# One pass of all 512 tokens up to the gates, in place of a pass of 128 tokens and a pass of 384

## The chip, the cores and the metric

One NeuronCore of one Trainium2 chip runs the whole layer. The metric is the device time of one execution in microseconds (us); of several runs the median counts.

## The reference

One layer of a streaming encoder, 512 tokens, model width 2048, all in float32:

```
h      = rms_norm(x)
proj   = h @ w_in                    # conv value, conv gate, q, k, v, gate_conv, gate_attn
conv   = silu(layer_norm(depthwise31(value * sigmoid(gate)))) @ w_conv_out
attn   = band_attention(rms(q), rms(k), v, rel_bias) @ w_attn_o
x      = x + (sigmoid(gate_conv) * conv + sigmoid(gate_attn) * attn) @ w_out
h2     = rms_norm(x)
idx, g = top 16 of 128 x 128 product keys, 8 heads, of h2 @ w_query
x      = x + sum_k g_k * gelu(h2 . expert_u[idx_k]) * expert_v[idx_k]
```

The convolution is causal over 31 taps, and the attention looks back 8 chunks of 64 tokens, so later tokens need values of earlier ones.

## The kernel before

The weights are streamed as some 640 pieces (**subs**) of 512 rows by 512 columns (1 MB) or 384 columns (0.75 MB, q, k and v of one head). `Net.run` goes through them in one order: for sub i it issues the load of a later sub on SP (tile `raw`), splits sub i+1 into a rounded high part `whi` (ACT, L121) and the rest `wlo` (DVE, L122), and issues the matmuls of sub i (`mm_sub`, L156): weight high by activation high, high by low, and low by high, 48 matmuls for one 1 MB sub where the tokens are the moving columns (`add_fm`), 12 where 128 tokens stand still and the weight's 512 columns move (`add_tm`). Behind each sub it pops background work from a queue with a budget: convolution taps, top-k, routing (`run_bg`), and **gather steps** from a second queue `gq` at a rate per sub (`grate`). A gather step fetches 128 rows of 8 KB of `expert_u` or `expert_v` with an indirect DMA on POOL (L1295) and then multiplies or accumulates them on DVE (L1322, L1330). There are 384 of them: 256 for the first 128 tokens, 128 for the last 64. The 320 tokens between go another way: all of `expert_u` and `expert_v` is streamed as weights (`ut`, `vt`).

The stages in program order:

- A, 128 tokens, 192 subs: convolution input (up to L428), q, k and v with plain float32 matmuls on weights that aren't split (`native`, L342), gates, then conv_out, attn_o, w_out and the query projection (L561 to L641). Its weight loads use five buffers, two of them in the pool `wpx` (L104), and run up to five subs ahead (L135).
- B, the other 384 tokens, 192 subs: b (convolution input), c (q, k, v and the attention, 16 heads), d (gates), e (conv_out), f (attn_o), g (w_out), i (query). The convolution's last 30 inputs and the keys and values of A come back through `cy_d` and `kv_d`. From here on three raw buffers are used. The top-k and routing of the first 128 tokens run in the background of b and c, and their gathers follow.
- k: `expert_u` by 320 tokens, 128 subs, with the routing of those tokens beside it (`place`, L1252, and `g_d`).
- m: `expert_v` by 320 tokens, 128 subs, with two 640 KB loads (`gt`, `gel`) for each four subs; then `finish_x` (L1344 on).

What `gq` still holds behind the last sub is run there, before `finish_x`:

```python
    N.run()
    while N.gq:
        N.gq.popleft()()
    finish_x()
```

Of the kernel before, what the change touches and what calls it, by code (L numbers as in the profile page):

```python
# [11 lines left out]
F32 = mybir.dt.float32  # L12
# [11 lines left out]
P = 128  # L24
# [19 lines left out]
UPB = 7  # L44
BUD_B = 4.4
BUD_C = 3.2
# [3 lines left out]
G_B, G_C, G_D, G_E, G_I, G_K, G_M = 0.4, 0.5, 1.1, 1.6, 0.6, 1.05, 1.15  # L50
URATE = 1.15
BUD_A, BUD_N = 0.5, 2.3
# [8 lines left out]
class Net:  # L61
    def __init__(self, nc, tc, A):
        self.nc, self.tc, self.A = nc, tc, A
        self.bg, self.late = deque(), deque()
        self.gq = deque()
        self.uq = deque()
        self.gacc, self.grate, self.credit, self.uacc = 0.0, G_B, 0.0, 0.0
        self.subs = []
# [22 lines left out]
    def add(self, src, ncol, mm, pre=None, post=None, budget=8.0, native=False):  # L91
        self.subs.append((src, ncol, mm, pre, post, budget, native))

    def run(self):
# [7 lines left out]
        def load(i):  # L102
            src, ncol = self.subs[i][:2]
            pool, bufs = (self.wpx, 2) if i < self.na and i % 5 > 2 else (self.wp, 3)  # L104
            raw = pool.tile([P, 4, ncol], F32, tag="raw", name="raw", bufs=bufs)
            for a, b in pieces(i):
                if i == 0:
                    self.beside(a)
                nc.sync.dma_start(raw[:, a:b, :], src[:, a:b, :])
            raws[i] = raw  # L110

        def split(i):
            raw = raws.pop(i)
            ncol = self.subs[i][1]
            if self.subs[i][6]:
                splits[i] = (raw, None)
                return
# [10 lines left out]
        for i in range(n):  # L128
            src, ncol, mm, pre, post, budget, native = self.subs[i]
# [57 lines left out]
def build(nc, tc, A):  # L187
# [4 lines left out]
    gp = es.enter_context(tc.tile_pool(name="gp", bufs=1))  # L192
    actp = []
# [4 lines left out]
    def act_tile(name):  # L198
        return actp[-1].tile([P, 4, T], F32R, tag="act", name=name, bufs=8)
# [23 lines left out]
    cy_d = drp.tile([P, 16, PAD], F32, name="cy_d")  # L223
    kv_d = [drp.tile([P, 4, 4, TA], F32, name=f"kvd{g}") for g in range(4)]
# [33 lines left out]
    def resplit(src4, goff, kg, rinv, new, name, n=T):  # L258
# [30 lines left out]
    io128f = gp.tile([P, 4, W], F32, tag="gat", name="io128f", bufs=3)[:, 0, :P]  # L289
# [17 lines left out]
    def blocks(t):
        return t.rearrange("p a (b c) -> p (a b) c", b=4)

    def wtmp(name):  # L310
        return pa.tile([P, W], F32, tag="wt", name=name, bufs=2)

    def small(n):
        return lambda name: pa.tile([P, n], F32, tag=f"{name}{n}", name=name, bufs=2 if n < TA else 1)

    nop = lambda: None

    def quad(c):
        return slice(4 * c, 4 * c + 4)

    def turned(src, then):

        def go():
            bank = psx.tile([P, 4, P], F32, tag="aux", name="tq", bufs=3)
            for k in range(4):
                nc.tensor.transpose(bank[:, k, :], src[:, k * P:k * P + P], ident)
            then(bank)
        pend.extend((nop, go))

    def add_tm(src, act, evac, nchunk, ncol=W, pre=None, budget=BUD_A, native=False, post=None):  # L330

        st = {}
        for c in range(nchunk):
            for kg in range(KG):
                def mm(hi, lo, c=c, kg=kg):
                    if kg == 0:
                        st[c] = psa.tile([P, W], F32, tag="acc", name="acc", bufs=5)
                    out = st[c][:, :ncol]
                    if native:
                        a = act()  # L340
                        for k in range(4):
                            ins = nc.tensor.matmul(out, a[:, kg * 4 + k, :], hi[:, k, :], start=kg == 0 and k == 0,  # L342
                                                   stop=kg == 3 and k == 3)
                            N.last_mm = getattr(ins, "ins", ins)
                        if kg == 3:
                            evac(c, out)
                        return
                    ah, al = act()
                    N.mm_sub([(lambda k: (hi[:, k, :], lo[:, k, :]),
                               lambda k: (ah[:, kg * 4 + k, :], al[:, kg * 4 + k, :]), out)],  # L350
                             kg == 0, kg == 3, lambda i: evac(c, out), swap=True)

                def after(c=c, kg=kg):
                    if pend:
                        pend.popleft()()
                    if post:
                        post(c, kg)
                N.add(src(c, kg).rearrange("p (k n) -> p k n", k=4), ncol, mm,
                      (lambda c=c, kg=kg: pre(c, kg)) if pre else None, after, budget, native)


    XA = {"f": blocks(gat("xaf"))}
    XA["t"] = gp.tile([P, 4, W], F32, tag="hy", name="xat")
    XA["h"] = pair("hx")

    def load_xf(k0, k1):
        nc.sync.dma_start(XA["f"][:, k0:k1, :], A["xA"].rearrange("p (k t) -> p k t", k=16)[:, k0:k1, :])

    N.beside = lambda k: load_xf(k, k + 1)

    def split_x(kg):
        for k in range(4 * kg, 4 * kg + 4):
            nc.scalar.activation(XA["f"][:, k, :], XA["f"][:, k, :], AF.Copy, scale=vcol(V_G1, k))
            if kg == 0:
                split_into(XA["h"][0][:, k, :], XA["h"][1][:, k, :], XA["f"][:, k, :])
        if kg:
            split_into(*(t[:, quad(kg), :] for t in XA["h"]), XA["f"][:, quad(kg), :])

    def pre_ab(c, kg):
        if c == 0 and kg == 0:  # L380
            split_x(0)
            load_xf(4, 8)
        elif c == 0 and kg < 3:
            load_xf(4 * kg + 4, 4 * kg + 8)
        if c == 0 and kg == 1:
            nc.sync.dma_start(vec[:, V_DW:], A["vec"][:, V_DW:])
            nc.sync.dma_start(XA["t"], A["xt0"].rearrange("p (a b) -> p a b", a=4))

    def post_ab(c, kg):
        if c == 0 and kg < 3:  # L390
            split_x(kg + 1)
        if c == 0 and kg == 2:
            jk = gat("jka")
            ss = small(1)("ssq")
            nc.scalar.activation(jk, XA["t"], AF.Square, accum_out=ss)
            XA["r"] = rsqrt(small(1), ss, 1, scale=1.0 / D)

    def evac_ab(c, acc):
        j, val = divmod(c, 2)
        if not val:  # L400
            XA["sig"] = wtmp("sig")
            nc.scalar.activation(XA["sig"], acc, AF.Sigmoid, scale=XA["r"])
            return
        u = wtmp("u")
        nc.vector.scalar_tensor_tensor(u, acc, XA["r"], XA["sig"], op0=ALU.mult, op1=ALU.mult)

        def then(bank):
            up = pa.tile([P, 4, TA + PAD], F32, tag="upa", name="upa", bufs=4)
            nc.vector.memset(up[:, :, :PAD], 0.0)
            nc.scalar.copy(up[:, :, PAD:], bank)  # L410
            nc.gpsimd.dma_start(cy_d[:, quad(j), :], up[:, :, TA:])
            if j == 0:
                XA["cr"] = blocks(gat("cr"))
            for b in range(4):
                for a in range(0, TAPS, 4):
                    N.push(0.3 * min(4, TAPS - a), lambda b=b, a=a: taps_a(up[:, b, :], 4 * j + b, a, min(a + 4, TAPS)))
        turned(u, then)

    def taps_a(u, ch, a, b):
        r = XA["cr"][:, ch, :]  # L420
        for i in range(a, b):
            w = vcol(V_DW, ch * TAPS + i)
            if i == 0:
# [1083 lines left out]
```

## Time and profile before

| | |
|---|---|
| median of 3 runs (lowest to highest) | 4242.41 us (4241.9 to 4245.78) |
| the profiled execution, its own time | 4250.59 us |
| its span, first to last instruction | 4248.8 us |
| PE, DVE, ACT, POOL busy | 95%, 82%, 42%, 22% of the span |
| bytes moved | 1193 MB, 281 GB/s over the span |

The span's stages are read off by the first matmul of each stage's input tile: A from 0, b at 630.2, c at 908.2, d at 1424, e at 1712.6, k at 2291.2, m at 3331.2, its last matmuls at 4239. A matmul's own length overlaps the next one's, so what a matmul takes is the distance between two starts.

### The profile page before, as it was taken

The page shows a single profiled execution, that of the slowest core. Times are in us where ns is not written, and L with a number is a line of the kernel's source. Part 1 is how long each engine was busy: PE and PEld are TensorE (multiplying, and loading weights), DVE is VectorE, ACT ScalarE, POOL GpSimd, SP SyncE. Part 2 cuts the span into 40 slices and gives each one's busy share as a digit, 9 for nine tenths or more (in the row PEclk, how much of TensorE's full clock was granted, in tenths as well). Part 3 has the DMA queues.
Part 4 walks back from the last instruction along what each step waited for, and adds up shares of the span by engine and source line. Part 5 has one row for each costly group of instructions (what it writes and reads, how often), then busy time and mean ns, then how long its engine had stood idle before and what let it go on. Part 6 is the DMA issues. An engine that isn't in the chain of part 4 may idle for free. (4 is left out here: it accounts for less than half of the span.)

```text
span 4248.8 us, 60672 instructions
## 1 busy us (share of the span) xinstructions
PE 4048.5 (95%) x24506; PEld 3862.0 (91%) x24506; DVE 3468.5 (82%) x4542; ACT 1773.9 (42%) x2356; POOL 944.3 (22%) x484
## 2 busy tenths in 40 slices
PE   7999989989999999999989998989999999999999
PEld 6657869989999999999989998988999999999999
DVE  7957989999887675788879998977775898899973
ACT  6238764225555443222333335455552333333332
POOL 0000000000001023333411231223443344344510
PEclk9999999999999999999999999999999999999999
DMA  8888983334346578999955886888989999999963
GB/s 336 292 299 308 374 308 109 127 109 138 130 139 224 215 275 301 371 360 345 344 185 207 318 329 246 332 300 289 326 302 354 366 370 373 350 367 364 370 249 129
DMA packets 254858, 1193.00 MB, mean 281 GB/s; under 512 B 26816, under 2 KB 105344, under 8 KB 139376
## 3 DMA queue, kind: packets, MB, share of 16 engines
q1 hardware_dynamic: 121616, 709.67, 45.9%
q0 software_dynamic: 61728, 425.19, 25.8%
q10 hardware_dynamic: 71232, 54.26, 3.9%
q8 instruction: 192, 3.15, 0.3%
q14 instruction: 90, 0.74, 0.0%
HBM read 1120.55 MB, written 68.40 MB: 280 GB/s over the span
## 5 line engine op out<-in xcount | busy, mean ns | idle before, releaser
L121 ACT CAST whi<-raw 128x2048 fp32r<-128x2048 f32 (+2 forms) x579 | 1072.2, 1853 | 1725.7 <-PE acc L156 1524.5
L122 DVE TENSOR_TENSOR wlo<-raw,whi 128x2048 fp32r<-128x2048 f32 (+2 forms) x579 | 1282.2, 2217 | 427.1 <-ACT whi L121 359.1
L156 PE MATMUL acc<-hah,whi 128*128 128x320 f32 x2048 | 621.5, 317 | 44.9 <-ACT ge L1369 23.6
L156 PE MATMUL acc<-hal,whi 128*128 128x320 f32 x2048 | 614.7, 314 | 0.0
L156 PE MATMUL acc<-wh,whi 128*128 128x320 f32 x2048 | 603.3, 309 | 0.0
L156 PE MATMUL acc<-wl,whi 128*128 128x320 f32 x2048 | 603.2, 309 | 0.0
L1295 POOL DMA_INDIRECT gat<-v,ix x128 | 289.4, 2261 | 755.7 <-DVE wlo L122 576.3
L156 PEld LDWEIGHTS acc<-hah,whi 128*128 128x128 f32 x2048 | 393.9, 192 | 47.5 <-ACT ge L1369 24.9
L1295 POOL DMA_INDIRECT gat<-u,ix x128 | 250.0, 1953 | 647.2 <-DVE wlo L122 555.1
L156 PEld LDWEIGHTS acc<-hal,whi 128*128 128x128 f32 x2048 | 393.5, 192 | 0.0
L156 PEld LDWEIGHTS acc<-wh,whi 128*128 128x128 f32 x2048 | 385.0, 188 | 0.0
L156 PEld LDWEIGHTS acc<-wl,whi 128*128 128x128 f32 x2048 | 384.7, 188 | 0.0
L156 PE MATMUL acc<-hah,wlo 128*128 128x320 f32 x2048 | 330.6, 314 | 10.4 <-DVE wlo L122 10.4
L156 PE MATMUL acc<-wh,wlo 128*128 128x320 f32 x2048 | 323.4, 310 | 3.5 <-DVE wlo L122 3.5
L1322 DVE SCALAR_TENSOR_TENSOR gat<-gat,xat 128x2048 f32<-128x2048 f32 x128 | 291.5, 2286 | 39.3 <-DMA gat<-u,ix 39.2
L156 PEld LDWEIGHTS acc<-hah,wlo 128*128 128x128 f32 x2048 | 312.4, 192 | 11.4 <-DVE wlo L122 11.4
L156 PEld LDWEIGHTS acc<-wh,wlo 128*128 128x128 f32 x2048 | 307.5, 189 | 4.0 <-DVE wlo L122 4.0
L156 PE MATMUL acc<-hh,whi 128*128 128x384 f32 x896 | 300.6, 336 | 2.1 <-ACT whi L121 1.2
L156 PE MATMUL acc<-hl,whi 128*128 128x384 f32 x896 | 300.2, 335 | 0.0
L1330 DVE SCALAR_TENSOR_TENSOR hy<-gat,wa,hy 128x2048 f32<-128x2048 f32 x128 | 300.0, 2344 | 0.1
L721 DVE SCALAR_TENSOR_TENSOR cacc<-upad,vec,cacc 128x384 f32<-128x384 f32 x480 | 277.5, 612 | 3.7
L156 PE MATMUL acc<-whi,hh 128*128 128x384 f32 x768 | 261.1, 340 | 6.4 <-DVE upad L711 6.3
(398 smaller groups left out, 7508.2 us busy)
## 6 DMA issues: line engine op xcount, KB each, us to landing
raw<-wfm SPq DMA_DIRECT2D x255, 1024.0 KB
raw<-ut SPq DMA_DIRECT2D x128, 1024.0 KB
raw<-vt SPq DMA_DIRECT2D x128, 1024.0 KB
raw<-wqkv SPq DMA_DIRECT2D x128, 768.0 KB
ged<-ge ACTq DMA_DIRECT2D x128, 160.0 KB
g_d<-sg ACTq DMA_DIRECT2D x20, 1024.0 KB
gt<-g_d SPq DMA_DIRECT2D x32, 640.0 KB
gel<-ged SPq DMA_DIRECT2D x32, 640.0 KB
```

The costliest lines, as they stand in the source:

```text
L121: nc.scalar.copy(hi[:, a:b, :], raw[:, a:b, :])
L122: ins = nc.vector.tensor_tensor(lo[:, a:b, :], raw[:, a:b, :], hi[:, a:b, :].bitcast(F32), op=ALU.subtract)
L156: ins = nc.tensor.matmul(out, *((a, w) if swap else (w, a)), **kw)
L721: nc.vector.scalar_tensor_tensor(r["a"], u[:, i:i + T], vcol(V_DW, ch * TAPS + i), r["a"], op0=ALU.mult, op1=ALU.add)
L1295: ins = nc.gpsimd.indirect_dma_start(out=t.rearrange("p a b -> p (a b)"), out_offset=None, in_=A[src], in_offset=bass.IndirectOffsetOnAxis ...
L1322: N.after_split(nc.vector.scalar_tensor_tensor(t, t, 1.0, S["u", who], op0=ALU.mult, op1=ALU.mult, accum_out=a[:, sl:sl + 1]))
L1330: N.after_split(nc.vector.scalar_tensor_tensor(y, t, S["w", who][:, sl:sl + 1], y, op0=ALU.mult, op1=ALU.add))
```

## The change

The kernel now takes all 512 tokens through b, c and d in one pass (tiles 512 wide, `open_acts(W)`, `n=W`; four token tiles per head in c). `cy_d`, `kv_d`, the plain float32 matmuls and the pool `wpx` are gone, and so are 128 subs: 32 of the convolution input, 64 of q, k and v, 32 of the gates. The gates of the first 128 tokens are turned by four transposes a chunk and kept in SBUF; the normalised convolution of the other 384 goes to DRAM (`s_d`) and comes back. Then conv_out, attn_o, w_out and the query projection run for 128 tokens (64 subs, `add_tm`), then e, f, g and i for 384 as before, then k and m. All loads use three buffers. The rates of the gathers change: 1.7 a sub in e, f and g (1.6 before), 0.8 in i (0.6), 0.9 in k (1.05), 1.35 in m (1.15), none before e (0.4, 0.5 and 1.1 in b, c and d). The core of the diff:

```diff
-G_B, G_C, G_D, G_E, G_I, G_K, G_M = 0.4, 0.5, 1.1, 1.6, 0.6, 1.05, 1.15
+G_E, G_I, G_K, G_M = 1.7, 0.8, 0.9, 1.35
...
-            pool, bufs = (self.wpx, 2) if i < self.na and i % 5 > 2 else (self.wp, 3)
-            raw = pool.tile([P, 4, ncol], F32, tag="raw", name="raw", bufs=bufs)
+            raw = self.wp.tile([P, 4, ncol], F32, tag="raw", name="raw", bufs=3)
...
-            while loaded < min(n, i + (5 if i + 4 < self.na else 3)):
+            while loaded < min(n, i + 3):
                 load(loaded)
...
-           evac_b, 8, pre=pre_b, post=post_b, budget=BUD_B)
+           evac_b, 8, pre=pre_b, post=post_b, budget=BUD_B, n=W)
...
-                        st["acc"] = [psa.tile([P, W], F32, tag="acc", name="acc", bufs=5) for _ in range(3)]
+                        st["acc"] = [psa.tile([P, W], F32, tag="acc", name="acc", bufs=5) for _ in range(4)]
...
+    def pre_ae(c, kg):
+        if c == 0 and kg == 0:
+            while pend:
+                pend.popleft()()
+            N.run_bg(1e9, late=False)
+            esF.close()
+            esAct.close()
+            S["gp"] = esG.enter_context(tc.tile_pool(name="gp", bufs=1, side="right"))
+            SA["p2"] = esA2.enter_context(tc.tile_pool(name="pa2", bufs=1))
+            SA["t"] = S["gp"].tile([P, 4, W], F32, tag="hy", name="xat")
+            nc.sync.dma_start(SA["t"], A["xt0"].rearrange("p (a b) -> p a b", a=4))
...
+    add_tm(lambda c, kg: A["wfm"][(16 + c) * 4 + kg], lambda: SA["s"], evac_ae, 4, pre=pre_ae)
...
+    add_tm(lambda c, kg: A["wfm"][(28 + c) * 4 + kg], lambda: SA["x1"], evac_ai, 4, pre=pre_ai)
...
     add_fm(lambda c, kg: A["wfm"][(16 + c) * 4 + kg], lambda c, kg: S["sa"][kg], evac_e, 4,
-           pre=pre_e, post=post_split("oa", lambda kg: S["o"][kg], 4), budget=4.0)
+           pre=pre_e, post=post_split("oa", lambda kg: S["o"][kg], 4), budget=5.5)
```

POOL's queue, from the last convolution writes (`u2d`) to the first gathers, before (L729 and L1024 write `u2d` and `x1d`, L1295 is a gather):

```order
L729 DMA u2d_86<-cacc 128x384 x4
L729 DMA u2d_87<-cacc 128x384 x4
L729 DMA u2d_88<-cacc 128x384 x4
L729 DMA u2d_89<-cacc 128x384 x4
L1295 DMA gat<-u,ix 128x2048 x106
L1024 DMA x1d_102<-x_15989 128x384 x4
```

and in the change (L683 fetches the first 128 tokens' attention, L709 the keys, L716 writes their new x, L1137 is a gather):

```order
L558 DMA s<-u2d_89 128x2048
L683 DMA of<-od_102 128x4x128
L683 DMA of<-od_103 128x4x128
L683 DMA of<-od_104 128x4x128
L683 DMA of<-od_105 128x4x128
L739 DMA g2row<-g 128x512
L709 DMA kraw<-keysT 128x256
L716 DMA xa_d<-xat 128x512 x4
L739 DMA g2row<-g 128x512 x3
L1137 DMA gat<-u,ix 128x2048 x50
L866 DMA x1d_106<-x_14235 128x384 x4
```

Before, 106 gathers stand ahead of the first write of g's result; now 50 do, and none stands ahead of the 128 tokens' own stages. By DVE's steps between two splits, the stages c, d, e, f, g, i, k and m held 12, 33, 25, 26, 25, 9, 132 and 122 gather steps before; now e, f, g, i and k hold 13, 27, 27, 14 and 114, and 189 are left for m and what follows it.

DVE at the end of the program, before (L122 splits a weight, L1431 adds an accumulator into the output):

```order
L1431 TENSOR_TENSOR y_28266<-acc,y_28266 128x320 x4
L122 TENSOR_TENSOR wlo<-raw,whi 128x2048 x2
L1431 TENSOR_TENSOR y_28267<-acc,y_28267 128x320 x4
L122 TENSOR_TENSOR wlo<-raw,whi 128x2048 x2
L1431 TENSOR_TENSOR y_28268<-acc,y_28268 128x320 x4
L122 TENSOR_TENSOR wlo<-raw,whi 128x2048
L1431 TENSOR_TENSOR y_28269<-acc,y_28269 128x320 x4
```

and in the change (L118 splits, L1172 is a gather step, L1273 adds an accumulator):

```order
L118 TENSOR_TENSOR wlo<-raw,whi 128x2048
L1172 SCALAR_TENSOR_TENSOR hy<-gat,wx,hy 128x2048 x2
L1273 TENSOR_TENSOR y_26471<-acc,y_26471 128x320 x4
L118 TENSOR_TENSOR wlo<-raw,whi 128x2048
L1172 SCALAR_TENSOR_TENSOR hy<-gat,wx,hy 128x2048 x4
L1273 TENSOR_TENSOR y_26472<-acc,y_26472 128x320 x4
L1172 SCALAR_TENSOR_TENSOR hy<-gat,wx,hy 128x2048 x17
```

Before, the last gather step lies 20 splits ahead of the end; now 17 of them stand behind the last output's additions.

SP's queue of loads in the change, from the convolution input to the end of the 128 tokens' stages (L108 loads a weight, L679 the first 128 tokens' x, L769 `s_d`):

```order
L108 DMA raw<-wfm 128x2048 x28
L108 DMA raw<-wqkv 128x1536 x64
L108 DMA raw<-wfm 128x2048 x36
L679 DMA xat<-xt 128x2048
L108 DMA raw<-wfm 128x2048 x56
L769 DMA sb<-sd_90 128x4x384
L108 DMA raw<-wfm 128x2048
L769 DMA sb<-sd_91 128x4x384
```

The load of `xat` goes into a pool that lies over the activations of d, and 56 weight loads stand behind it; before, it was issued near the start of the program.

## Rows read from the trace of the kernel before

**Rows 1.** The page's parts 1 and 4: busy time by engine, the chain by engine.
```profile
PE 4048.5 (95%) x24506; PEld 3862.0 (91%) x24506; DVE 3468.5 (82%) x4542; ACT 1773.9 (42%) x2356; POOL 944.3 (22%) x484
...
PE 28%; DMA 2%; ACT 1%; ACTq 0%; DVE 0%; issue 0%; SPq 0%; DVEq 0%
```

**Rows 2.** Busy time by stretch, one row a stage; conv_out of 128 tokens last.
```profile
core 0: us, PE busy (x) PEld busy (x) DVE busy (x) ACT busy (x) POOL busy (x), PEclk, DMA share, GB/s
0.00:119.60 119.60, 96.09 (x393) 74.06 (x394) 91.61 (x100) 80.29 (x74) 5.33 (x14) 0.97 0.90 331
119.60:308.60 189.00, 181.06 (x630) 110.51 (x628) 148.28 (x516) 46.59 (x141) 9.53 (x16) 0.99 0.84 291
308.60:422.60 114.00, 103.59 (x486) 83.20 (x485) 85.77 (x56) 92.82 (x93) 2.16 (x4) 0.99 0.81 312
422.60:630.20 207.60, 191.28 (x866) 154.24 (x864) 180.60 (x175) 143.84 (x113) 4.33 (x8) 0.97 0.91 346
630.20:908.20 278.00, 272.34 (x1538) 270.61 (x1539) 264.34 (x495) 93.41 (x100) 3.25 (x6) 0.98 0.35 124
908.20:1424.00 515.80, 484.65 (x2834) 473.48 (x2834) 436.30 (x809) 262.87 (x590) 24.24 (x25) 0.98 0.45 155
1424.00:1712.60 288.60, 277.68 (x1590) 275.06 (x1589) 184.51 (x176) 116.42 (x143) 74.47 (x33) 0.98 0.74 274
1712.60:2291.20 578.60, 559.66 (x3218) 555.79 (x3217) 474.52 (x662) 178.86 (x180) 176.99 (x113) 0.98 0.80 302
2291.20:3331.20 1040.00, 974.28 (x6813) 959.91 (x6813) 849.70 (x939) 480.55 (x764) 314.73 (x144) 0.96 0.85 311
3331.20:4091.00 759.80, 756.29 (x5137) 755.76 (x5136) 683.05 (x558) 237.31 (x139) 329.27 (x121) 1.00 0.95 365
4091.00:4241.00 150.00, 150.00 (x1016) 148.96 (x1015) 69.76 (x67) 39.27 (x23) 0.00 (x0) 1.00 0.39 140
422.60:466.10 43.50, 43.50 (x193) 36.02 (x192) 38.17 (x20) 31.21 (x18) 0.00 (x0) 1.00 0.98 387
```

**Rows 3.** Groups by line, busy us, mean ns: the plain float32 matmuls of q, k and v.
```profile
L342 PE MATMUL acc<-raw,xaf 128*128 128x384 f32 x512 | 169.6, 490 | 0.0
```

**Rows 4.** Timeline of PE: start, length; 512 columns, first and last of 8.
```profile
449.78 0.39 PE L156 MATMUL acc<-whi,sah 128*128 128x512 f32 x1
...
451.37 0.39 PE L156 MATMUL acc<-whi,sal 128*128 128x512 f32 x1
```

**Rows 5.** Timeline of PE: 384 columns, first and last of 31.
```profile
900.05 0.33 PE L156 MATMUL acc<-hl,whi 128*128 128x384 f32 x1
...
905.25 0.33 PE L156 MATMUL acc<-hl,whi 128*128 128x384 f32 x1
```

**Rows 6.** Timeline at the start: SP's first loads, ACT's first split, PE's first matmul.
```profile
0.76 2.77 SPq L109 DMA_DIRECT2D raw<-wfm  x6
...
4.47 0.62 ACT L121 CAST whi<-raw 128x512 fp32r<-128x512 f32 x1 [2.23 <-DMA raw<-wfm]
...
15.41 0.80 PE L156 MATMUL acc<-whi,hxh 128*128 128x512 f32 x1 [15.41 <-ACT hxh L240]
```

**Rows 7.** Groups by line, shapes apart: the two splits of a 1 MB sub.
```profile
L122 DVE TENSOR_TENSOR wlo<-raw,whi 128x2048 fp32r<-128x2048 f32 x511 | 1167.3, 2287 | 406.6 <-ACT whi L121 345.3 <-PE acc L156 29.4 <-ACT ge L1369 10.8
L121 ACT CAST whi<-raw 128x2048 fp32r<-128x2048 f32 x511 | 975.2, 1910 | 1589.9 <-PE acc L156 1427.3 <-issue 44.4 <-DMA raw<-ut 23.9
```

**Rows 8.** Groups by line: a gather step on DVE and its issue on POOL.
```profile
L1330 DVE SCALAR_TENSOR_TENSOR hy<-gat,wx,hy 128x2048 f32<-128x2048 f32 x64 | 150.1, 2346 | 3.9 <-DMA hy<-xx_d 3.7
...
L1295 POOL DMA_INDIRECT gat<-v,ixx x64 | 182.8, 2856 | 215.7 <-DVE wlo L122 212.0 <-issue 3.4 <-DVE y L1431 0.3
```

**Rows 9.** Busy time by stretch, columns as in rows 2: m's first and last with gathers.
```profile
3331.00:3500.00 169.00, 165.49 (x1109) 164.96 (x1108) 151.88 (x137) 51.66 (x33) 72.99 (x28) 0.98 0.97 374
...
3900.00:4091.00 191.00, 191.00 (x1304) 191.00 (x1303) 174.83 (x130) 60.61 (x35) 80.83 (x28) 1.00 0.94 360
```

**Rows 10.** Timeline of DVE at the end: the last output's additions.
```profile
4237.45 2.25 DVE L1431 TENSOR_TENSOR y<-acc,y 128x320 f32<-128x320 f32 x4 [9.63 <-PE acc L156]
```

More of the change, by code (lines that the diff above doesn't have):

```diff
@@ L128, in run @@
         for i in range(n):
-            src, ncol, mm, pre, post, budget, native = self.subs[i]
+            src, ncol, mm, pre, post, budget = self.subs[i]
             self.now = i
@@ L310, in wtmp @@
[L310 to L359, printed above, removed]
@@ L362, in build @@
[L362 to L377, printed above, removed]
@@ L398, in evac_ab @@
[L398 to L417, printed above, removed]
@@ L511, in build @@
-    add_tm(lambda h, kg: A["wqkv"][h * 4 + kg], lambda: XA["f"], evac_ac, NH, ncol=384, pre=pre_ac, native=True,
-           budget=BUD_N)
-    def pre_ad(c, kg):
-        if kg == 3 and c == 0:
-            while pend:
-                pend.popleft()()
-            esAt.close()
-            XA["sg"] = esAs.enter_context(tc.tile_pool(name="sga", bufs=1, side="right")).tile([P, 8, W], F32, name="sg")
-        if kg == 0 and c == 2:
-            N.run_bg(1e9)
-            pend.extend(norm_a())
-    def sum_blocks(src):
-        ps = psx.tile([P, TA], F32, tag="aux", name="mua", bufs=3)
-        for b in range(16):
-            nc.tensor.matmul(ps, ones, src[:, b, :], start=b == 0, stop=b == 15)
-        return ps
@@ L883, in build, with blocks, quad @@
     add_c()
-    esL, esH = ExitStack(), ExitStack()
-    esS = ExitStack()
+    esL, esH, esS, esF, esA1 = (ExitStack() for _ in range(5))
+    SA = {}
+    def blocks(t):
+        return t.rearrange("p a (b c) -> p (a b) c", b=4)
+    def quad(c):
+        return slice(4 * c, 4 * c + 4)
     def fl(name):
@@ new lines, in wtmp, with small, turned, go @@
+    def wtmp(name):
+        return SA["p2"].tile([P, W], F32, tag="wt", name=name, bufs=2)
+    def small(n):
+        return lambda name: SA["p2"].tile([P, n], F32, tag=f"{name}{n}", name=name, bufs=2 if n < TA else 1)
+    def turned(src, then):
+        def go():
+            bank = psx.tile([P, 4, P], F32, tag="aux", name="tq", bufs=3)
+            for k in range(4):
+                nc.tensor.transpose(bank[:, k, :], src[:, k * P:k * P + P], ident)
+            then(bank)
+        pend.extend((nop, go))
@@ new lines, in add_tm, with mm, after @@
+    def add_tm(src, act, evac, nchunk, ncol=W, pre=None, budget=BUD_A, post=None):
+        st = {}
+        for c in range(nchunk):
+            for kg in range(KG):
+                def mm(hi, lo, c=c, kg=kg):
+                    if kg == 0:
+                        st[c] = psa.tile([P, W], F32, tag="acc", name="acc", bufs=5)
+                    out = st[c][:, :ncol]
+                    ah, al = act()
+                    N.mm_sub([(lambda k: (hi[:, k, :], lo[:, k, :]),
+                               lambda k: (ah[:, kg * 4 + k, :], al[:, kg * 4 + k, :]), out)],
+                             kg == 0, kg == 3, lambda i: evac(c, out), swap=True)
+                def after(c=c, kg=kg):
+                    if pend:
+                        pend.popleft()()
+                    if post:
+                        post(c, kg)
+                N.add(src(c, kg).rearrange("p (k n) -> p k n", k=4), ncol, mm,
+                      (lambda c=c, kg=kg: pre(c, kg)) if pre else None, after, budget)
@@ new lines, in load_s, with pre_ai, end_a @@
+    def load_s(kg):
+        SA["sb", kg] = gat("sb")[:, :, :T]
+        nc.sync.dma_start(SA["sb", kg], s_d[kg])
+    def pre_ai(c, kg):
+        if c == 2 and kg > 1:
+            load_s(kg - 2)
+        if c == 3:
+            if kg == 0:
+                S["sa"] = []
+            S["sa"].append(split_act(SA.pop(("sb", kg)), "sa"))
+            if kg < 2:
+                load_s(kg + 2)
+    add_tm(lambda c, kg: A["wfm"][(28 + c) * 4 + kg], lambda: SA["x1"], evac_ai, 4, pre=pre_ai)
+    def end_a():
+        while pend:
+            pend.popleft()()
+        esA2.close()
+        esA1.close()
+        S["u", "a"] = SA["t"]
```

527 lines of the change are left out of this document (209 added, 318 removed).

## Prediction

> **What bounds the kernel now.** I read the shares of the engines first, then the busy time stage by stage, then single steps in the timeline. PE is busy for 95% of the span, and what the chain of waits names is PE for the most part [rows 1]. So the question of each stage is whether PE waits there, and for what. The table by stages [rows 2] shows four kinds. In the 128-token stages (the first four rows, 630 us) PE's busy time is 24, 8, 10 and 16 us short of the stretch, the DMA queues are 81 to 91% busy, and in the second the plain float32 matmuls of q, k and v alone are busy for 170 us [rows 3]. In b, c and d (1082 us) PE is nearly always busy and DMA is at 35 to 74%. In e to i and in k, DMA is at 80 and 85%, and PE idles for 19 and 66 us. In m, as long as there are gathers (760 us), PE is busy for 756 of them, while DVE is at 683 and DMA at 95%; the last 150 us of m have no gathers and DMA falls to 39%. The reader should see that this kernel keeps PE full by spreading 384 gathers over the stages from c on. The change takes work from the first kind of stage and pushes gathers into the last.
>
> **The change, part by part.** All sums are made against the profiled execution (span 4248.8 us, own time 4250.6); the median, 4242.4, is 8 us under it, and I carry the difference over to the median.
>
> *b, c and d in one pass.* PE streams the same columns; what goes is time in which PE waited, and the plain float32 matmuls (170 us [rows 3], where split ones would be 64 x 12 x 0.1733 = 133). A 512-column matmul steps by 1.59 / 7 = 0.227 us [rows 4], a 384-column one by 5.20 / 30 = 0.1733 us [rows 5]. New: 64 subs x 48 x 0.227 = 697 us for b and d, 64 x 48 x 0.1733 = 532 us for c. Before, the 384 tokens' own matmuls were 64 x 48 x 0.1733 + 64 x 36 x 0.1733 = 932 us of 1082, so 151 us were attention and waits. Of these, 485 - 399 = 85 us are attention matmuls in c [rows 2]; ten key blocks for nine and eight transposes for six make them about 1.15 times as long: +13. The chain from one attention step to the next is not shortened, so I keep the rest of the 151. The gates' 32 transposes add about 5. The first matmul can hardly start earlier than at 15.4 us [rows 6], and a clock of 0.97 in the first 120 us [rows 2] is worth 4. Together 15 + 697 + 532 + 151 + 13 + 5 + 4 = 1417 us to the end of d. Bounds: the 151 can fall to some 110 if DVE, rid of gathers and top-k in c, answers at once, and grow by a third if the longer tiles wait longer: 1375 to 1465.
>
> *The 128 tokens' second half, 64 subs.* On PE it is 64 x 12 x 0.227 = 174 us, and before it took 207.6 us [rows 2], with the first 16 subs at PE's pace of 2.72 us and DMA at 98%, 387 GB/s [rows 2]. Two of the five raw buffers are gone. A buffer is filled in about 5.7 us (3.7 us from the issue of the first quarter to its use [rows 6], and the other 0.75 MB at 387 GB/s) and emptied by both splits one after the other, 1.91 + 2.29 us [rows 7]: with three buffers one sub each (5.7 + 4.2) / 3 = 3.3 us, more than PE's 2.72. The load of `xat` waits for the last matmul of d, and the third sub's weight stands behind it on SP: that weight lands about 3 us and 3 MB later (xat and the attention's 1 MB share the queues), and PE, covered for 5.4 us by two subs, idles some 8. So 5 + 8 + 62 x 3.3 = 218, and 15 for the reload of `s_d`, its splits and the last scores: 233 us. Bounds: 215 (three buffers are enough) and 255 (3.6 us a sub). The page "DMA: Bandwidth & Descriptors" of the Trainium skill, section "Anatomy of one DMA — SWDGE (gpsimd) path", gives an estimate of 2.0 us and bytes / 436 GB/s for one transfer; by it a fill would take 4.4 us and a sub 2.9, and this term would be some 25 us less; the first load of this trace took longer, and I go by it.
>
> So e starts at 1417 + 233 = 1650 us in place of 1712.6: **-63 us** (-123 to +7 with all bounds, which don't fall together).
>
> *e, f, g, i.* 81 gather steps in place of 85, but e now also carries the top-k and routing of the first 128 tokens, which ran in b and c, under a budget of 5.5. DVE was busy for 475 of 579 us [rows 2]. I take **+8** (0 to 15).
>
> *k.* 18 gather steps fewer, 18 x 2.35 = 42 us of DVE time [rows 8] in a stage where PE idles for 66 us [rows 2], for the most part behind other chains: **-8** (-20 to 0).
>
> *m and the gathers behind it.* This term decides. Before, m took 760 + 150 = 910 us [rows 2], 7.11 us a sub. Now 189 gather steps are left for it instead of 122, 17 of them behind the last addition. The bytes from m's start to the end: 128 weights of 1.049 MB (134), 64 loads of 0.655 MB (42), 189 gathers of 1.049 MB (198), 5 for y and the output, less 6.5 loaded ahead: 373 MB. At 1.35 gathers a sub m would need 2.79 MB in 7.11 us, 392 GB/s. With gathers, m moved 374 GB/s at 97% of the queues' time where it moved most, and 360 where least [rows 9]. I take 374, the rate of this mix at its fullest stretch, in which PE already idled for 3.5 us: 373 / 0.374 = 997 us, 3 us for the last step on DVE: 1000, or **+90 us**. Lower bound: PE keeps 7.11 us a sub and the 17 steps follow at DVE's 2.35 us [rows 8], 910 + 40 = 950 (+40); POOL's 2.86 us for one issue would make the 17 steps 49. Upper bound: 373 / 0.360 = 1036 (+126). The Trainium skill, page "DMA: Bandwidth & Descriptors", section "Where 436 GB/s comes from", puts what HBM serves one core at about 358 GB/s; by it this term would be 373 / 0.358 = 1042 us, +132. The 374 and 387 GB/s of these rows are above it, so it is not taken. DVE is no bound of its own: it was busy for 683 + 70 us in m [rows 2], 122 x 2.35 = 287 of them gather steps; with 172 steps it would be 870 of 910. What follows the gathers (`finish_x`, 8 us behind the last addition [rows 10]) is unchanged.
>
> Sum: -63 + 8 - 8 + 90 = +27 us. 4248.8 + 27 = 4276 us of span, and at the median 4242.4 + 27 = **4269 us**, 0.6% slower. A difference under 0.2% (8.5 us) can't be told from none here.
>
> **The rivals.**
>
> *DMA keeps up in m (faster).* PE keeps its pace in m, and only the 17 steps at the end are new: -63 + 8 - 8 + 40 = -23, 4219 us. For it: conv_out of 128 tokens drew 387 GB/s without a wait on PE [rows 2], and m was never starved at 365. Against it: the queues were already at 95 to 97% there [rows 2, 9], so 392 asks for more than they have left; it needs 373 MB in 950 us, 393 GB/s. It decides where the queues of m deliver over some 390. The Trainium skill's page "DMA: Bandwidth & Descriptors", section "Where 436 GB/s comes from", gives 435 GB/s as the ceiling of the fabric, by which m would not be bound by DMA at all; no stretch of this trace comes near it, the most is 387. Chance 0.25.
>
> *The two sides cancel (same).* m moves 384 GB/s, which is its 365 at 95% carried to 100% [rows 2]: 971 + 3 = 974, +64, and the sum is +1: 4243 us. Chance 0.17.
>
> *The 128 tokens starve (slower by more).* A sub there takes 3.6 us or a longer gap opens at its start (+22), and m falls back to 360 GB/s (+36): 4327 us. DMA at 97% with three buffers speaks for it; that e to i ran with three buffers without loss speaks against it. Chance 0.13.
>
> That the change doesn't do what it says is ruled out by the order of the instructions: no gather step stands ahead of the 128 tokens' own stages, and 17 stand behind the last addition.
>
> **How the numbers follow.** The forecast has 0.45, the rivals 0.25, 0.17 and 0.13. Slower by over 0.2%: 0.45 + 0.13 = 0.58; within: 0.17; faster: 0.25. The range runs from 4205 (the first rival with a front 14 us better) to 4325 (the last rival); about 0.08 lies below it and 0.09 above. The forecast's own range is 4251 to 4295.
>
> **What would show it.** The first matmul of e should start near 1650 us, of k near 2230, of m near 3260. The stage of 64 subs should show some 230 us and ACT's casts waiting for `raw`, with a gap on PE behind the third sub's weight. m should show DMA at 97% or more, PE busy for clearly less than its stretch, and splits that wait for `raw` of `vt`; behind the last addition there should be 17 gather steps, some 2.4 to 2.9 us apart. I am wrong if m keeps 7.1 us a sub with 1.35 gathers in it, or if e starts later than 1690 or earlier than 1610.

## The result and the profile after

The changed kernel takes 4197.53 us (median of 4 runs, 4193.86 to 4205.79) where the kernel before, run beside it, takes 4244.09 (4241.9 to 4249.36). The ratio is 0.9891, with a 95% interval of 0.9874 to 0.9909: 1.1% faster, where 0.6% slower was forecast. The profiled execution has a span of 4204.0 us, 44.8 us less than before.

Parts 1 and 4 of the page after, the lines that answer to [rows 1]:

```profile
PE 4003.9 (95%) x23898; PEld 3775.8 (90%) x23898; DVE 3282.0 (78%) x3969; ACT 1623.1 (39%) x2230; POOL 958.8 (23%) x501
...
PE 21%; DMA 4%; issue 3%; POOL 2%; DVE 1%; ACT 1%; ACTq 0%; POOLq 0%; DVEq 0%; SPq 0%
```

PE is busy for 45 us less in a span that is 45 us shorter. The chain now runs over DMA and POOL too: part of that are the gathers behind the last matmul.

Busy time by stretch of the kernel after, one row a stage as in [rows 2]: b, c, d, the 64 subs of the 128 tokens, e to i, k, m, and what follows m.

```profile
core 0: us, PE busy (x) PEld busy (x) DVE busy (x) ACT busy (x) POOL busy (x), PEclk, DMA share, GB/s
0.00:378.00 378.00, 361.38 (x1538) 290.81 (x1539) 274.27 (x342) 106.32 (x108) 5.82 (x16) 1.00 0.32 114
378.00:1000.00 622.00, 621.08 (x3708) 614.99 (x3707) 480.59 (x805) 301.39 (x725) 21.10 (x39) 1.00 0.30 100
1000.00:1374.60 374.60, 371.42 (x1609) 298.44 (x1608) 126.58 (x129) 129.77 (x174) 3.80 (x7) 0.99 0.36 127
1374.60:1600.30 225.70, 203.93 (x854) 150.58 (x853) 180.38 (x156) 146.50 (x118) 7.88 (x13) 0.98 0.90 324
1600.30:2194.90 594.60, 565.68 (x3216) 559.20 (x3215) 509.64 (x865) 177.43 (x177) 168.38 (x111) 0.97 0.78 292
2194.90:3226.20 1031.30, 971.67 (x6830) 957.08 (x6830) 815.30 (x982) 482.94 (x767) 261.02 (x124) 0.97 0.82 296
3226.20:4141.00 914.80, 903.61 (x6146) 902.56 (x6144) 853.70 (x676) 276.41 (x160) 463.30 (x177) 1.00 0.98 387
4141.00:4204.00 63.00, 5.18 (x8) 2.08 (x8) 41.51 (x22) 2.31 (x4) 27.47 (x14) 0.56 0.73 265
```

The reader should take three things from it. In b, c and d PE idles for 16.6, 0.9 and 3.2 us, the first of them the start of the program. In m the queues deliver 387 GB/s over the whole stage, and PE is busy for 904 of 915 us. And behind m stand 63 us of which PE is busy for 5.

| term | forecast | measured |
|---|---|---|
| end of d | 1417 | 1374.6 |
| the 128 tokens' 64 subs | 233 | 225.7 |
| start of e, against 1712.6 before | -63 | -112.3 |
| e, f, g, i (578.6 before) | +8 | +16.0 |
| k (1040.0 before) | -8 | -8.7 |
| m and all behind it (917.6 before) | +90 | +60.2 |
| sum | +27 | -44.8 |

Two terms failed, the end of d by 42 us and m by 30.

What PE waited for (us in all, times, longest) in b to d before, the five largest (the one for `xgh` ends with b's first matmul and so lies in the stage ahead of b), and then from the start to the end of d after, all rows:

```profile
PE acc L156 <- DVE wlo L122: 12.2, 2, 8.1
PE tr L786 <- DVE qk L780: 12.0, 14, 1.8
PE vp L928 <- issue: 8.8, 1, 8.8
PE acc L156 <- ACT xgh L253: 7.2, 1, 7.2
PE acc L156 <- DVE upad L711: 6.3, 1, 6.3
```

```profile
PE acc L152 <- ACT whi L117: 16.6, 1, 16.6
PE acc L152 <- ACT ga L602: 3.2, 1, 3.2
PE tr L419 <- issue: 0.9, 1, 0.9
```

The waits of the attention are gone but for 0.9 us at one transpose: those for `qk` (the scaled q and k of a head, 14 of 16 heads) and one of 4.1 us for the normalised scores. The longer ones behind `wlo` and `upad` are gone too. That is the gain the forecast left out.

DVE behind the last additions of m, after (`y` is the last output; columns: start, length, engine, line, operation, and in brackets the idle time before it and what ended it):

```profile
4140.95 1.68 DVE L1273 TENSOR_TENSOR y<-acc,y 128x320 f32<-128x320 f32 x4
4142.55 7.12 DVE L1172 SCALAR_TENSOR_TENSOR hy<-gat,wx,hy 128x2048 f32<-128x2048 f32 x3
4150.77 2.35 DVE L1172 SCALAR_TENSOR_TENSOR hy<-gat,wx,hy 128x2048 f32<-128x2048 f32 x1 [1.10 <-DMA gat<-v,ixx]
...
4190.34 2.35 DVE L1172 SCALAR_TENSOR_TENSOR hy<-gat,wx,hy 128x2048 f32<-128x2048 f32 x1 [0.39 <-DMA gat<-v,ixx]
```

The 17 steps take (4192.7 - 4142.6) / 17 = 2.95 us each: DVE's own 2.35 [rows 8], and waits for the gathers.

### The profile page after: what moved, and what is told of

It reads as the page before. It is cut to its first block, busy times and chain, and to the rows that moved or that the text cites. A ratio compares the mean times of both kernels' runs of the same rounds, so it can differ in the third digit from the quotient of the medians.

```text
span 4204.0 us, 58198 instructions
## 1 busy us (share of the span) xinstructions
PE 4003.9 (95%) x23898; PEld 3775.8 (90%) x23898; DVE 3282.0 (78%) x3969; ACT 1623.1 (39%) x2230; POOL 958.8 (23%) x501
## 5 line engine op out<-in xcount | busy, mean ns | idle before, releaser
L117 ACT CAST whi<-raw 128x2048 fp32r<-128x2048 f32 (+2 forms) x515 | 951.1, 1847 | 1928.6 <-PE acc L152 1692.2
L118 DVE TENSOR_TENSOR wlo<-raw,whi 128x2048 fp32r<-128x2048 f32 (+2 forms) x515 | 1137.8, 2210 | 609.0 <-PE acc L152 349.4
L1137 POOL DMA_INDIRECT gat<-v,ix x128 | 351.9, 2749 | 582.1 <-DVE wlo L118 561.7
L1137 POOL DMA_INDIRECT gat<-u,ix x128 | 223.9, 1749 | 721.2 <-DVE wlo L118 372.3
L360 DVE SCALAR_TENSOR_TENSOR cacc<-upad,vec,cacc 128x512 f32<-128x512 f32 x480 | 358.4, 750 | 10.3
L152 PE MATMUL acc<-hh,whi 128*128 128x512 f32 x896 | 354.8, 396 | 3.2 <-ACT ga L602 3.2
L152 PE MATMUL acc<-hl,whi 128*128 128x512 f32 x896 | 357.0, 398 | 0.0
L152 PE MATMUL acc<-whi,hh 128*128 128x384 f32 x1024 | 347.2, 339 | 0.0
L152 PE MATMUL acc<-whi,hl 128*128 128x384 f32 x1024 | 344.1, 336 | 0.0
```

The costliest lines, as they stand in the source:

```text
L117: nc.scalar.copy(hi[:, a:b, :], raw[:, a:b, :])
L118: ins = nc.vector.tensor_tensor(lo[:, a:b, :], raw[:, a:b, :], hi[:, a:b, :].bitcast(F32), op=ALU.subtract)
L152: ins = nc.tensor.matmul(out, *((a, w) if swap else (w, a)), **kw)
L360: nc.vector.scalar_tensor_tensor(r["a"], u[:, i:i + W], vcol(V_DW, ch * TAPS + i), r["a"], op0=ALU.mult, op1=ALU.add)
L1137: ins = nc.gpsimd.indirect_dma_start(out=t.rearrange("p a b -> p (a b)"), out_offset=None, in_=A[src], in_offset=bass.IndirectOffsetOnAxis ...
```

## The experiments

**The rates alone, on the kernel before.** Two passes as before, the gathers as in the change.

```diff
-G_B, G_C, G_D, G_E, G_I, G_K, G_M = 0.4, 0.5, 1.1, 1.6, 0.6, 1.05, 1.15
+G_B, G_C, G_D, G_E, G_I, G_K, G_M = 0.0, 0.0, 0.0, 1.7, 0.8, 0.9, 1.35
```

> The kernel before with the change's rates alone: no gathers in b, c and d, 1.7 in e to g, 0.8, 0.9 and 1.35 after; two passes as before. 176 gather steps are left for m, 4 behind the last addition. Theory A (PE waited in c and d because DVE was busy with gather steps): PE's waits in b to d fall from 48 us to under 10, e starts near 1670, k is 8 us shorter, m keeps 7.12 us a sub, the end costs 12: about 4205 us. Theory B (what removed the waits is the 512-token pass, in which one sub gives the attention chain 8.3 us where it had 6.2): e starts near 1705, about 4240 us.

Measured: 4254.35 us, ratio 1.0019 (1.0008 to 1.0031), where the forecast by A was 4205 and by B 4240. Busy time by stretch of this kernel, c, d and m:

```profile
911.00:1420.50 509.50, 482.78 (x2836) 472.29 (x2835) 407.97 (x784) 263.23 (x591) 5.40 (x10) 0.99 0.38 128
1420.50:1695.20 274.70, 274.48 (x1588) 273.10 (x1587) 112.42 (x110) 113.74 (x140) 0.00 (x0) 1.00 0.46 164
...
3307.20:4221.00 913.80, 904.23 (x6146) 902.68 (x6144) 852.91 (x675) 276.08 (x160) 463.23 (x176) 1.00 0.98 387
```

Without gathers d loses all its idle time (10.9 us before, 0.2 now), and c hardly any: 31.2 before, 26.7 now, the 12.1 us for `qk` among them. What d lost is for the most part one wait, the 8.8 us for `vp`: before, the layer norm's last sum, which `vp` reads, stood behind gather steps on DVE. So A holds for d and fails for c. The last row settles the question of m by itself: the same stage of the same kernel, which moved 365 GB/s over its 760 us with gathers [rows 2], moves 387 at the higher rate, and PE keeps its 7.1 us a sub. The 374 of [rows 9] was near what m asked for (1.05 + 0.33 + 1.15 x 1.05 = 2.58 MB in 7.11 us, 363 GB/s), not what the queues could give. The gain in front (e starts 17 us earlier) is given back behind: with 176 gather steps for 122, m and all behind it take 940 us for 918.

**Longer subs, on the kernel before.**

```diff
-                        st["acc"] = [psa.tile([P, W], F32, tag="acc", name="acc", bufs=5) for _ in range(3)]
+                        st["acc"] = [psa.tile([P, W], F32, tag="acc", name="acc", bufs=5) for _ in range(4)]
...
+                        if tt == 3:
+                            return
...
-                               lambda k, tt=tt: (ah[:, k, tt * P:tt * P + P], al[:, k, tt * P:tt * P + P]),
-                               st["acc"][tt][:, :384]) for tt in range(3)], kg == 0, kg == 3, evac, swap=True)
+                               lambda k, tt=tt % 3: (ah[:, k, tt * P:tt * P + P], al[:, k, tt * P:tt * P + P]),
+                               st["acc"][tt][:, :384]) for tt in range(4)], kg == 0, kg == 3, evac, swap=True)
```

> The kernel before with 12 matmuls more in each sub of c (the first token tile's once again, into a fourth accumulator that nothing reads): a sub then lasts 48 x 0.1733 = 8.3 us on PE, as in the changed kernel, where it had 6.2, and nothing else changes. Added work: 64 x 12 x 0.1733 = 133 us. Theory B (the waits of c come from subs too short for the attention chain and the taps): PE's waits in c fall from 31 us to under 8, c takes about 516 + 133 - 25 = 624 us, the whole about 4352. Theory A (DVE's gathers in c make them): waits stay near 31, c takes 649 us, the whole about 4377.

Measured: 4355.68 us in one run. PE's waits in c, all rows, and the busy time of c:

```profile
PE acc L156 <- DVE upad L711: 10.1, 1, 10.1
PE acc L156 <- DVE wlo L122: 3.9, 1, 3.9
PE tr L786 <- DVE qk L780: 0.4, 1, 0.4
```

```profile
909.40:1535.00 625.60, 610.98 (x3604) 606.48 (x3603) 446.04 (x810) 268.62 (x594) 19.58 (x25) 0.99 0.38 129
```

The stage got 133 us more of matmuls and is 110 us longer (625.6 against 515.8), with the gathers still in it. The waits for `qk` and `sc` are gone but for 0.4 us; only two near the stage's start are left, 14 us for the forecast of under 8. So the wait inside c is one of length: an attention step has one sub's time to be answered, and 8.3 us are enough where 6.2 were not.

**Each attention step one sub later, on the kernel before.**

```diff
                         ss[0]()
+                        if h == 0:
+                            pend.append(lambda: None)
                         pend.extend(ss[1:])
```

> The kernel before with one empty step ahead of the first attention step of c, so that each step follows one sub later: the chain from a head's last accumulators to the transposes of its q and k (10.1 us where one head was read) has two subs of 6.2 us to run beside, not one. Theory B (the waits for qk come from short subs): the 12.0 us that PE waited for qk in 14 of the heads go; the waits at the stage's start stay; 4230 to 4234 us. Theory A (DVE is too busy there): they stay, or turn up behind the next step; 4240 to 4246.

Measured: 4265.67 us, ratio 1.0048 (1.0033 to 1.0064), slower than either theory said. The largest of PE's waits in b to d of this kernel, and that for `qk`:

```profile
PE trp L833 <- DVE sc L816: 21.5, 12, 5.4
...
PE tr L786 <- DVE qk L780: 0.2, 1, 0.2
```

The wait for `qk` went as B said, 12.0 to 0.2 us, and 12 times PE now waits one step on, for the normalised scores (4.1 us before, 21.5 now). One step got two subs, but the next still had one, and by the order of the program it now shares its sub with the following head's first step; that this makes its wait is argued, no run shows it apart. Giving one link more time moved the wait; with more time for every link (the run with longer subs, and the 512-token pass) it is gone. It doesn't speak for A, whose gathers were there in both.

**More gathers in k, and in m.** Each alone, on the changed kernel.

```diff
-G_E, G_I, G_K, G_M = 1.7, 0.8, 0.9, 1.35
+G_E, G_I, G_K, G_M = 1.7, 0.8, 1.05, 1.35
```

> The changed kernel with a rate of 1.05 gathers a sub in k in place of 0.9: 19 gather steps go from m and the end to k, none stands behind the last addition. Theory (the end is paid step by step: 17 steps behind the last addition took 4142.6 to 4192.7, 2.95 us each, and k has room on DVE, 815 of 1031 us busy): k 1031 to about 1036, m stays at 912, the last 57 us go; about 4145 us. Rival (k is not free: before, with 132 gathers, it took 1040, and each step put in delays the splits): k grows by 19 x 2.35 = 45 us and the time stays at 4185 to 4195.

```diff
-G_E, G_I, G_K, G_M = 1.7, 0.8, 0.9, 1.35
+G_E, G_I, G_K, G_M = 1.7, 0.8, 0.9, 1.5
```

> The changed kernel with a rate of 1.5 gathers a sub in m in place of 1.35, so that all of them end before the last sub. A sub of 7.12 us then asks for 1.05 + 0.33 + 1.57 = 2.95 MB, 414 GB/s, where m drew 387 on average and 407 at most. Theory (the queues still have room and DVE is the next bound: 3.7 us a sub without gathers + 1.5 x 2.35 = 7.2): m grows by at most 15 us, the end of 57 goes, about 4150 us. Rival (387 was nearly all that the queues give): 373 MB at 390 GB/s are 956 us, PE waits for raw, about 4185 us.

Measured: 4159.21 us, ratio 0.9800 (0.9781 to 0.9819), and 4159.54, ratio 0.9788 (0.9769 to 0.9807). Busy time by stretch: k and m of the first, m of the second.

```profile
2184.20:3235.20 1051.00, 980.12 (x6831) 963.85 (x6830) 858.13 (x1002) 483.35 (x768) 324.94 (x144) 0.96 0.85 310
3235.20:4142.00 906.80, 903.04 (x6141) 902.78 (x6140) 848.38 (x675) 276.25 (x160) 449.93 (x172) 1.00 0.97 386
```

```profile
3221.80:4148.00 926.20, 904.97 (x6140) 901.72 (x6140) 887.80 (x693) 276.95 (x160) 410.15 (x190) 0.99 0.99 399
```

The end of the program goes in both, as the theory had it (4145 and 4150 us forecast, 4185 and more by the rivals). A step in k costs about 1 us of the span here (20 us for 19), between the theory's 0.3 and the rival's 2.35. That price is one execution's: with 114 to 116 steps k took 1028.6 to 1036.0 us in six runs of this record, and in the kernel before some 18 steps more made it 7 to 10 us longer. In m the queues now carry 399 GB/s over 926 us, and from its first matmul to its last the stage grows by some 15 us. DVE is busy for 888 of the 926, so this run alone doesn't tell whether the loads or DVE set it.

**Where the queues end.** Gather steps of half the width in m.

```diff
-G_E, G_I, G_K, G_M = 1.7, 0.8, 0.9, 1.35
+G_E, G_I, G_K, G_M = 1.7, 0.8, 0.9, 1.8
...
+        c = slice(0, 2 if N.grate == G_M else 4)
...
-            N.after_split(nc.vector.scalar_tensor_tensor(y, t, S["w", who][:, sl:sl + 1], y, op0=ALU.mult, op1=ALU.add))
+            N.after_split(nc.vector.scalar_tensor_tensor(y[:, c], t[:, c], S["w", who][:, sl:sl + 1], y[:, c], op0=ALU.mult, op1=ALU.add))
```

> The changed kernel with a rate of 1.8 gathers a sub in m, where each gather step on DVE takes 1024 of the 2048 columns (the rest of the products is left out): DVE then needs 3.7 + 1.8 x 1.2 = 5.9 us of 7.12 a sub and sets nothing, while the queues are asked for 1.05 + 0.33 + 1.89 = 3.27 MB a sub, 459 GB/s. Theory (the queues' own end lies well above the 374 that the forecast took): in the first 104 subs they show 100% of their time and over 410 GB/s, PE waits for raw, and m is no longer than some 930 us. Rival (about 400 is the end): those 104 subs take 104 x 3.27 / 0.4 = 850 us in place of 741, m some 1020.

Measured: 4248.66 us in one run. Busy time of m while it has gathers:

```profile
3217.70:4090.00 872.30, 784.36 (x5146) 778.18 (x5146) 628.27 (x624) 237.12 (x139) 260.77 (x189) 0.95 0.99 398
```

What PE waited for in m, then what ACT's casts waited for from `raw`, and what DVE waited for, the two largest:

```profile
PE acc L152 <- DVE wlo L118: 88.2, 22, 13.8
```

```profile
ACT whi L117 <- DMA raw<-vt: 188.2, 30, 11.2
```

```profile
DVE gel L1253 <- DMA gel<-ged: 77.7, 17, 10.2
DVE gat L1165 <- DMA gat<-u,ixx: 51.1, 27, 5.3
```

The rival is right here: asked for 459 GB/s, the queues give 398, m takes 1020 us, and PE idles for 88 us. DVE is busy for 628 of 872 us and sets nothing by itself; it stands still for loads (of `gel` and of gathers), and ACT's casts stand still for `raw`. PE's own waits are all for `wlo`, the split behind both, where the first theory had named `raw`. So this mix of loads ends at about 400 GB/s; what sets that end no run takes apart. The change asks for 392, just under it; that is why m kept its pace.

**Five raw buffers for the 128 tokens.**

```diff
-            raw = self.wp.tile([P, 4, ncol], F32, tag="raw", name="raw", bufs=3)
+            pool, bufs = (self.wpx, 2) if self.n0 + 2 <= i < self.n1 and i % 5 > 2 else (self.wp, 3)
+            raw = pool.tile([P, 4, ncol], F32, tag="raw", name="raw", bufs=bufs)
...
-            while loaded < min(n, i + 3):
+            while loaded < min(n, i + (5 if self.n0 <= i and i + 4 < self.n1 else 3)):
...
```

> The changed kernel with two more raw buffers for conv_out, attn_o and w_out of the 128 tokens (48 subs), loads five subs ahead there. Theory (the ring of three buffers sets that stage, about 3.4 us a sub): those 48 subs come down to PE's 2.8 us a sub, the stage from 226 to about 200 us, in all about 4172 us. Rival (the stage waits for the rate of the queues, which are at 90%): 0 to 5 us, 4193 to 4198.

Measured: 4187.52 us, ratio 0.9862 (0.9844 to 0.9879). The attn_o stage of the 128 tokens (16 subs) by stretch, after and with five buffers:

```profile
1430.20:1482.00 51.80, 49.34 (x204) 35.67 (x204) 42.55 (x26) 31.92 (x19) 0.55 (x1) 1.00 0.90 325
```

```profile
1426.40:1471.30 44.90, 44.90 (x205) 37.19 (x204) 42.24 (x27) 32.32 (x20) 0.55 (x1) 1.00 0.97 364
```

What ACT's casts waited for from attn_o to the end of w_out (32 subs), the largest row after and with five buffers:

```profile
ACT whi L117 <- DMA raw<-wfm: 33.5, 29, 2.2
```

```profile
ACT whi L118 <- PE acc L153: 16.0, 21, 0.8
```

With three buffers a sub takes 51.8 / 16 = 3.24 us and the casts wait for loads; with five it takes 2.81, PE's pace, and they wait for PE. The ring set that stage, as the forecast's 3.3 us said. The whole stage falls from 225.7 to 207.7 us and the span of the profiled execution by 17.5. The median falls by 10, where the theory had 25 and the rival 0 to 5; the profiled execution of the change was the longest of its four.

**e with less background work.**

```diff
-           pre=pre_e, post=post_split("oa", lambda kg: S["o"][kg], 4), budget=5.5)
+           pre=pre_e, post=post_split("oa", lambda kg: S["o"][kg], 4), budget=4.0)
```

> The changed kernel with a budget of 4.0 in place of 5.5 for background work in e: the top-k of the first 128 tokens spreads into f, 8 gather steps in e where there were 13, 22 behind the last addition where there were 17. Theory (e is 12 us longer than before because DVE, 126 of 146 us busy, answers late): e comes down from 146 to about 140 us and the end grows by 5 x 2.95 = 15 us; about 4207 us. Rival (e waits for loads of the gates and attention, not for DVE): e stays at 146, about 4212.

Measured: 4205.83 us in one run. Busy time of e, after and with the smaller budget, and DVE's gather steps in it, after and with the smaller budget:

```profile
1600.30:1746.80 146.50, 138.26 (x785) 137.08 (x784) 126.50 (x285) 39.21 (x25) 26.17 (x15) 0.97 0.77 286
```

```profile
1602.90:1740.70 137.80, 137.78 (x786) 137.22 (x785) 114.38 (x272) 39.18 (x25) 14.26 (x10) 1.00 0.68 250
```

```profile
L1164 DVE SCALAR_TENSOR_TENSOR gat<-gat,xat 128x2048 f32<-128x2048 f32 x14 | 31.9, 2289 | 15.5 <-DMA gat<-u,ix 15.5
```

```profile
L1164 DVE SCALAR_TENSOR_TENSOR gat<-gat,xat 128x2048 f32<-128x2048 f32 x8 | 18.2, 2289 | 4.4 <-DMA gat<-u,ix 4.4
```

e takes 137.8 us where it took 146.5, and PE no longer idles there, where it did for 8.2 us. But the top-k did not move into f, as was expected: its instructions in e are the same, one for one, in both runs. What left e is six gather steps (five by the order of the instructions), and 22 of them stand behind the last addition for 17, which takes back what e gained. So e's idle time came of top-k and gather steps together on DVE, and fewer gather steps were enough to end it. f takes 144.8 us for 140.2 with the same 6.0 us of idle PE; the rest is busy time at a mean granted clock of 0.96, where it was 1.00.

**The edits together.** Five buffers, `xat` on POOL's queue, and rates of 0.98 in k and 1.42 in m; then the same with the budget of 4.0 in e and other rates.

```diff
...
-            nc.sync.dma_start(SA["t"], A["xt0"].rearrange("p (a b) -> p a b", a=4))
+            nc.gpsimd.dma_start(SA["t"], A["xt0"].rearrange("p (a b) -> p a b", a=4))
...
-G_E, G_I, G_K, G_M = 1.7, 0.8, 0.9, 1.35
+G_E, G_I, G_K, G_M = 1.7, 0.8, 0.98, 1.42
```

> Three edits on the changed kernel together: five raw buffers as in the run of that alone, the load of xat on POOL's queue and not on SP's, rates of 0.98 in k and 1.42 in m (124 and 179 gather steps, none behind the last addition). Theory (the parts add up): the end goes (-38 to -40 net, as with either rate alone), five buffers give -10 to -18, the gap of 5.9 us behind the third sub of conv_out shrinks or goes: about 4140 us. Rival (xat on POOL's queue only moves the gap, since the bytes share the queues, and five buffers pull loads that meet it): 4145 to 4150.

> The run with five raw buffers, xat on POOL's queue and moved rates, with a budget of 4.0 in e and rates of 1.0 in i and k and 1.45 in m: 8 gather steps in e, 17 in i, 127 in k, 178 in m. Theory (e gives 7 us back, as in the look at that budget alone, and the 2 to 3 steps more in i and k cost 1 us each): about 4136 us. Rival (a gather step costs DVE the same 1 us wherever it goes and e's gain is lost in f, as e there gave 9 and f took 4): 4139 to 4143.

Measured: 4141.51 us (4136.47 to 4145.43), ratio 0.9757 (0.9744 to 0.9770), and 4145.91 (4134.96 to 4149.29), ratio 0.9759 (0.9746 to 0.9773). The parts add up: this is 2.4% under the kernel before and 56 us under the change. The last step adds nothing that these runs can tell: in its profiled execution e is 8.9 us shorter than in the run without it, and f and i together 9.2 longer. The load of `xat` on another queue gave little: the gap near the start of the 128 tokens' stages is still PE's longest wait there, 4.5 us where it was 5.1 with five buffers alone and 5.9 in the change.

## Why the prediction was wrong

Both of its signs of being wrong came: m kept 7.1 us a sub with 1.35 gathers in it, and e started at 1600.3, earlier than 1610.

**The end of d (1417 forecast, 1374.6 measured).** The step that failed is "The chain from one attention step to the next is not shortened, so I keep the rest of the 151." The chain indeed isn't shorter: in a head of c, from the first copy of its q and k to the scaled ones, it took 10.1 us before and 11.3 after. But the cover became longer, and the 151 held 47.7 us of PE waits (5.7, 31.2 and 10.9 in b, c and d, [rows 2]) that I didn't take apart. After the change b to d hold 4.1 us of waits besides the start. The difference, 43.6, is the miss of 42.4, but for the start (16.6 us for 15). The forecast saw that the 151 could fall and set the lower bound of 1375 by it, for another reason (DVE rid of gathers and top-k), which the run without gathers, which kept the top-k, bears out for d and not for c.

The rest of the sum held: streaming, attention and gates come to 1374.6 - 16.6 - 4.1 = 1353.9 us, and the forecast's terms without its waits and its start to 1417 - 15 - 47.7 = 1354.3. That is in part luck: c's 621 us of busy PE are some 10 under its terms (532 + 85 + 13), and b's and d's 733 are some 9 over theirs (697 + 5 + 4 and the 18 that b and d had beside streaming before).

Of the 43.6, 30 are in c, 8 in d and 6 in b. In c about 17 are the longer subs (31.2 to 14.6 in the run with longer subs alone); d's went in the run without gathers. The 14 us near c's start and the 6 in b no run isolates. For those of c the trace of the kernel before shows what they stood behind (DVE's taps of the convolution and the split after them, then PE's first matmul behind that split):

```profile
914.35 15.96 DVE L721 SCALAR_TENSOR_TENSOR cacc<-upad,vec,cacc 128x384 f32<-128x384 f32 x30
...
931.69 1.75 DVE L122 TENSOR_TENSOR wlo<-raw,whi 128x1536 fp32r<-128x1536 f32 x1
```

```profile
933.50 3.76 PE L156 MATMUL acc<-wlo,hh 128*128 128x384 f32 x12 [8.14 <-DVE wlo L122]
```

Thirty taps in a row stand ahead of that split, and 26 more, 13.9 us, ahead of the next `upad`, for which PE waits 6.3 us. The kernel before runs pending taps at once when all its `upad` buffers are taken (the loop at L707, `UPB = 7`). The change has ten buffers and no such loop, which the list of its parts above leaves out, and at most six taps in a row near c's start. So those 14 us most likely went by a part of the change that is neither the wider tiles nor the rates; that is read from the order of the instructions. The largest wait of b, 4.1 us for `wlo` at 708, stands behind the first 128 tokens' top-k on DVE, which the change moved to e.

**The 128 tokens (233, measured 225.7).** Right in the main: 3.24 us a sub in attn_o and 3.4 in w_out for the forecast's 3.3, with the ring of three buffers as its cause. The gap was forecast behind two subs, at 8 us, for the third sub's weight behind `xat` on SP. It measured 5.9 and stands behind the fourth sub: SP's queue has four loads of the stage ahead of `xat` (36 in that row, of which d has 32), and the fifth was issued 2.4 us behind it, when a split had freed its buffer. ACT stood still for 6.9 us ahead of its cast of the attention (`of`), for a DMA, with the fifth weight's cast behind that. So the size came near in part by luck. Behind the gap the granted clock is 0.51 for 4.8 us, which is the lower of the two levels (1.2 GHz), after 5.9 us in which PE did nothing.

**e to i (+8, measured +16).** Right in kind and mis-sized: e alone is 12 us longer than before; it now holds the top-k of the first 128 tokens beside gather steps, and in the budget run, with the same top-k and fewer gather steps, PE's 8.2 us of idle time there are gone. **k (-8, measured -8.7).** Right.

**m and behind it (+90, measured +60.2).** The step that failed is "I take 374, the rate of this mix at its fullest stretch". At 97% of the queues' time I read a stage at its end; it was a stage that asked for no more. The trace of the kernel before already held higher rates, against the forecast's "the most is 387"; its m with gathers in 40 slices of 19 us, in GB/s:

```profile
GB/s 396 357 390 370 381 381 365 393 336 392 347 370 376 358 385 358 366 357 358 309 341 362 376 351 420 354 380 379 356 351 366 349 363 398 404 313 370 371 366 302
```

Single slices reach 404 and 420. m draws 387 GB/s with a share of 0.98, 399 with 0.99 when asked for 414, and 398 with 0.99 when asked for 459. The rival that DMA keeps up put its point of decision at some 390 GB/s, and the queues' end turned out to be about 400. That rival was the right mechanism for m, with a chance of 0.25, and its lower bound of +40 was too low for another reason: 17 steps at 2.35 us were counted, and each took 2.95, with DVE waiting for gathers six times, 9 us in all; that is 10 of the 20 us between. Another 8 lie in m up to its last addition, with four gather steps between the last split and that addition, and 2 in what follows the gathers.

The Trainium skill, page "DMA: Bandwidth & Descriptors", section "Where 436 GB/s comes from", gives about 358 GB/s as what HBM serves one core, and 435 as the fabric's ceiling. The runs stand between: 398 and 399 GB/s over 870 and 926 us. The Trainium skill, page "HBM Reference", section "Specifications (TRN2)", says that a core which streams alone measures well above its share, about 425 GB/s; by that the 358 is no bound for a kernel on one core, and m agrees with it.

## What to carry to other kernels

A wait inside a stage is a term of its own: when the tile grows, take the stage apart into work and waits, and ask of each wait whether the work that covers it grew, before keeping it. A high share of the queues' busy time doesn't show what the queues can deliver; only a stretch in which something waits for its load does. And work that spreads behind others is cheapest when it ends just before they do: 17 gather steps cost 50 us behind the last stage, and about 1 us each or less inside k and m.

## What the runs showed that was not expected

- The share of the queues' busy time went from 0.95 to 0.99 while the rate of m went from 365 to 399 GB/s, so near its top the share says little. In m the limit for these loads was about 400 GB/s; the fullest stretch of 200 us had 415 (3600 to 3800 of the run with 1.5 in m).
- When the loads came late, PE never waited for `raw` itself: in the run with half steps its 88 us of waits are all for `wlo`, with DVE standing still for `gel` and gathers ahead of the splits, and ACT for `raw` (188 us).
- Delaying one link of the attention chain made the kernel 0.5% slower, and only 8.6 of the 17 us that c grew are idle time of PE; the other 8.6 are busy time, at a mean granted clock of 0.97 in that stage where it was 0.98 [rows 2].
